# Routing of the gathered tile moved into the loop, and the early dot products read from PSUM behind their gathers

## The chip, the cores and the metric

The kernel runs on one core of one Trainium2 chip. The metric is the device time of one execution in microseconds, the median of three runs. The engines are named as the profile names them: PE (TensorE), DVE (VectorE), ACT (ScalarE), POOL (GpSimd), SP (which issues most transfers).

## The reference, cut to what matters

One layer of an encoder on 512 tokens of width 1024: a mixer (gating and banded attention), then a layer of 16384 experts of one row each, called PEER. All is float32. The change is in PEER:

```python
def block(xb):                                   # 128 tokens
    q = (xb @ w_query).reshape(128, 8, 2, 128)
    sc = einsum('thpd,hpkd->thpk', q, sub_keys)  # 8 heads, 2 halves, 128 keys
    s_top, i_top = top_k(sc, 16)
    cand = s_top[:, :, 0, :, None] + s_top[:, :, 1, None, :]
    cand_idx = i_top[:, :, 0, :, None] * 128 + i_top[:, :, 1, None, :]
    best, pos = top_k(cand.reshape(128, 8, 256), 16)
    eidx = take_along_axis(cand_idx.reshape(128, 8, 256), pos)
    g = softmax(best)
    h = gelu(einsum('thkd,td->thk', expert_u[eidx], xb))
    return einsum('thk,thkd->td', g * h, expert_v[eidx])
```

So each token chooses 16 of 16384 experts in each of 8 heads (the routing), and its output is a sum over 128 experts.

## The kernel before

The 512 tokens are four tiles of 128. The kernel treats the experts in two ways. For tiles 1 to 3 it multiplies all 16384 experts, in 64 chunks of 256: a first product (expert rows by tokens, then gelu, `first_products`, two units a chunk), a factor that is zero where an expert wasn't chosen (the gates), and a second product that accumulates in PSUM (`second_product`). For tile 0 it gathers the 128 chosen rows of each token from `expert_u` and `expert_v` with indirect transfers (`gather_u`, `gather_v`) and multiplies on DVE. The last 64 tokens of tile 3 are a mixture: their first products are left out of the matmuls and come from 64 gathers of `expert_u` (two heads of 64 tokens share one gather of 128 rows), the early dot products of `gather_early`. Their operand is `xbu`, their results go to `du`. Every float32 matrix product is three products of split operands: `load_split` loads `raw`, ACT rounds it to `hi`, DVE or POOL subtracts to get `lo`.

After the mixer (to about 236 us) the work runs in three stages:

1. Routing, one head at a time (`candidates`, `choose`): the query product and the scores on PE, then on DVE for each tile and half a `top16` (two rounds of the eight largest with their places), the candidate sums, another `top16` over 50 candidates, and a selection by predicated copies from `tree`, whose mask stands in PSUM. POOL makes the `lo` of the query weights, some small index operations and the copy `tree`. Each head also holds one chunk of first products. From the fourth head's pass on, three early gathers a pass are issued.
2. The gates stage: 48 steps of 8 tokens. A step makes two one-hot matrices: `bm` on DVE, multiplied by the gates on POOL, and `am` on DVE (even steps) or on ACT (odd ones). Two steps later PE multiplies them, ACT copies the result to `gst`, and every four steps 2 MB go to DRAM (`gd`). The remaining early gathers are spread over the first `SOON` = 28 steps, and units of the first product fill PE's time.
3. The loop over 64 chunks: the second product of chunk c, the first of c + 19, and tile 0's 256 gathers with their work on DVE, spread in proportion. The gates come back from `gd` as `gc`.

Instructions are written in program order; a scheduler then orders those of each engine by priority and by when its own model has their inputs ready, except PE's in the gates stage and the loop, which keep program order. Once built, every engine executes its list in order. A tile of a pool with n buffers waits until the last user of the one n back is done: the early gathers write `rowe`, with three buffers. PSUM has eight banks: two for `pu` (first products), six for `pa` (all others, six accumulators in the loop). In before, a dot product follows its gather at once:

Of the kernel before, what the change touches and what calls it, by code (L numbers as in the profile page):

```python
# [58 lines left out]
ROWE = 3  # L59
# [8 lines left out]
PRIO = 400  # L68
GB = 4
# [10 lines left out]
def hybrid_block(tc, x, ln1, w_in, gng, wsT, bsb, qkg, bias, w_out, ln2, wq, skT, uT, ud, vd, out):  # L80
    nc = tc.nc
    ctx = ExitStack()
    with ctx:
# [3 lines left out]
        ps_a = ctx.enter_context(tc.tile_pool(name="ps_a", bufs=6, space=PSUM))  # L87
# [343 lines left out]

        rt = ctx.enter_context(tc.tile_pool(name="rt", bufs=1, side="right"))
# [10 lines left out]
        xbu = gat.tile([P, D], F32, name="xbu")  # L443
        for i in range(P // UX):
            nc.sync.dma_start(xbu[i * UX:(i + 1) * UX, :], xbd[1, P - UX:, :])
# [4 lines left out]
        early = []  # L450

        def gather_early(n):
            for j in early[:n]:
                row = gat.tile([P, D], F32, name="rowe", tag="rowe", bufs=ROWE)
                nc.gpsimd.indirect_dma_start(out=row, out_offset=None, in_=ud,  # L455
                                             in_offset=bass.IndirectOffsetOnAxis(ap=eui[:, j:j + 1], axis=0))
                nc.vector.scalar_tensor_tensor(row, row, 1.0, xbu, op0=ALU.mult, op1=ALU.mult,  # L457
                                               accum_out=du[:, j:j + 1])
# [35 lines left out]

        routing = ExitStack()
        rq = routing.enter_context(tc.tile_pool(name="rq", bufs=1))
        bits = rq.tile([P, 6], U32, name="bits")
        for i in range(6):
            nc.vector.memset(bits[:, i:i + 1], 1 << i)
# [8 lines left out]

        def candidates(h):
# [4 lines left out]

            top = rq.tile([P, 2, TT, 2, TOPK], F32, name="top", tag="top", bufs=2)
            pos = rq.tile([P, TT, 2, TOPK], U32, name="pos", tag="pos", bufs=2)
# [10 lines left out]
            next(fill, None)  # L527
            for p2 in range(2):
# [4 lines left out]
                sc = rq.tile([P, TT, NK], F32, name="scr", tag="scr", bufs=2)  # L533
                nc.scalar.copy(sc, sp.rearrange("p (t n) -> p t n", n=NK))
# [6 lines left out]
            nc.gpsimd.tensor_copy(top[:, 1, :, 1, :], pos[:, :, 1, :])  # L541
            cand = rq.tile([P, 2, TT, NCAND], F32, name="cand", tag="cand", bufs=2)
            a = top.rearrange("p a t q r -> p (a t) q r")
            c = cand.rearrange("p a t n -> p (a t) n")
            for i, j in ROWS:
                m, n = j - i, NPAIR[i]
                full = [P, 2 * TT, m, n]
                nc.vector.tensor_tensor(c[:, :, POFF[i]:POFF[i] + m * n].rearrange("p c (m n) -> p c m n", n=n),
                                        a[:, :, 1, None, 0:n].to_broadcast(full),
                                        a[:, :, 0, i:j, None].to_broadcast(full), op=ALU.add)  # L550
            return cand

        def choose(h, cand):

            hs = slice(h * TOPK, (h + 1) * TOPK)
            best = gate[:, :, hs]
            tree = rq.tile([P, TT, TOPK, 32], F32, name="tree", tag="tree", bufs=1)
            nc.gpsimd.tensor_copy(tree, cand[:, 1, :, None, 0:32].to_broadcast([P, TT, TOPK, 32]))
            bpos = rq.tile([P, TT, TOPK], U32, name="bpos", tag="bpos", bufs=2)
            for t in range(TT):  # L560
                rep = rq.tile([P, NCAND], F32, name="rep2", tag="rep2", bufs=2)
                top16(best[:, t, :], bpos[:, t, :], cand[:, 0, t, :], rep)

            mask = ps_a.tile([P, 512], U32, name="mask", tag="pa")[:, 0:6 * TT * TOPK]
            nc.vector.tensor_tensor(mask.rearrange("p (l n) -> p l n", l=6),
                                    bpos.rearrange("p t k -> p (t k)")[:, None, :]
                                    .to_broadcast([P, 6, TT * TOPK]),
                                    bits[:, :, None].to_broadcast([P, 6, TT * TOPK]), op=ALU.bitwise_and)
            mask = mask.rearrange("p (l t k) -> p l t k", t=TT, k=TOPK)
            for i in reversed(range(6)):  # L570
                if i == 5:
                    n = NCAND - 32
                    other = cand[:, 1, :, None, 32:NCAND].to_broadcast([P, TT, TOPK, n])
                else:
                    n = 1 << i
                    other = tree[:, :, :, n:2 * n]
                nc.vector.copy_predicated(tree[:, :, :, 0:n],  # L577
                                          mask[:, i, :, :, None].to_broadcast([P, TT, TOPK, n]), other)
            nc.gpsimd.tensor_copy(eidx[:, :, hs], tree[:, :, :, 0])
# [5 lines left out]
        for h in range(NH + 1):  # L585
            if h < NH:
                cands.append(candidates(h))
            gather_early(EARLY)
            if h > 0:
                choose(h - 1, cands.pop(0))  # L590
# [6 lines left out]
        best = gate.rearrange("p t (h k) -> p (t h) k", k=TOPK)  # L597
        full = [P, TT * NH, TOPK]
        ex = rq.tile(full, F32, name="ex")
        nc.vector.tensor_tensor(ex, best, best[:, :, 0:1].to_broadcast(full), op=ALU.subtract)  # L600
        nc.scalar.activation(ex, ex, AF.Exp)
        zs = rq.tile([P, TT * NH], F32, name="zs")
        nc.vector.reduce_sum(zs, ex, axis=AX.X)
        nc.vector.reciprocal(zs, zs)
        nc.vector.tensor_tensor(best, ex, zs[:, :, None].to_broadcast(full), op=ALU.mult)
        nc.vector.tensor_copy(eint, eidx[:, 0, :])
# [65 lines left out]
        hots, gs = {}, {}  # L672
        with tc.manual_schedule(engines={mybir.EngineType.PE}):
            for n in range(steps + LEAD):
                if n < steps:
# [3 lines left out]
                    hots[n] = one_hots(gs[t], c, n % 2 == 1)  # L679
                    want = (len(early) + max(0, SOON - n) - 1) // max(1, SOON - n)  # L680
                    gather_early(want)
                    if c == per - LEAD - 2 and t + 1 < ND:
                        if t + 2 == ND:
                            gather_early(len(early))
                            weights_early()
# [8 lines left out]
                while filled < min(last, 2 * (NH * FILL + 1) + (last - 2 * (NH * FILL + 1)) * (n + 1) // SOON):  # L694
# [152 lines left out]
```

## Time and profile before

| | |
|---|---|
| median of three runs | 1576.74 us (1573.69 to 1576.75) |
| profiled execution | 1577.37 us, of which its span 1575.3 |
| mean granted clock of PE | 0.955 |
| busy: PE, DVE, ACT, POOL | 1415.6, 1173.5, 652.6, 687.4 us |
| transfers | 394.66 MB, mean 251 GB/s |

Times in the profile count from the span's start. Busy time counts a pipelined instruction to its modelled end, so neighbours can overlap, and the distance between two starts says more than a duration. An idle time is put down to what ended it.

### The profile page before, as it was taken

To read this page: it belongs to the slowest core of one execution; us is meant where nothing else is said; L and a number is where in the kernel's file an instruction comes from. 1 tells how busy PE (TensorE), PEld (TensorE's weight loads), DVE (VectorE), ACT (ScalarE), POOL (GpSimd) and SP (SyncE) were. 2 spreads that over 40 slices of the span, in tenths; PEclk is the share of its full clock that TensorE was granted. 3 is DMA by queue.
4 is the path that set the end of the run, shared out by engine and by line. 5 is a ranking of instruction groups with operands and counts; after the bars stand their busy time and mean duration, and the time that the engine had idled before them with its cause. 6 is when DMAs were issued, how large, how long until landed. Compare 5 with 4: busy or idle time off the path is not lost.

```text
span 1575.3 us, 21612 instructions
## 1 busy us (share of the span) xinstructions
PE 1415.6 (90%) x7801; PEld 1249.5 (79%) x7801; DVE 1173.5 (74%) x2257; ACT 652.6 (41%) x1118; POOL 687.4 (44%) x464
## 2 busy tenths in 40 slices
PE   7999999987627666969999999999999999999988
PEld 6886779976527556868898998989999898988866
DVE  4437455999998878645787888888788788868774
ACT  5457443322125446963343333333333343333321
POOL 0000035675457664631445455555445554525320
PEclk9999999999759788999999999999999999999999
DMA  5352244265247886677999999999999999978872
GB/s 175 106 174 68 94 160 141 94 219 164 94 134 225 274 263 199 190 229 279 346 337 351 339 344 338 349 328 343 352 337 336 354 341 337 336 278 306 336 255 98
DMA packets 161210, 394.66 MB, mean 251 GB/s; under 512 B 11920, under 2 KB 72336, under 8 KB 161104
## 3 DMA queue, kind: packets, MB, share of 16 engines
q1 hardware_dynamic: 64912, 199.25, 36.6%
q0 software_dynamic: 46432, 168.60, 29.3%
q10 hardware_dynamic: 49760, 25.45, 5.7%
q8 instruction: 61, 1.00, 0.3%
q14 instruction: 45, 0.37, 0.1%
HBM read 362.81 MB, written 30.41 MB: 250 GB/s over the span
## 4 chain that ended last, share of the span: by engine, by line
PE 53%; DVE 8%; DMA 7%; issue 4%; ACT 3%; POOL 2%; DVEq 0%; SPq 0%; POOLq 0%; ACTq 0%
PE pa L774 10%; PE pa L775 10%; PE pa L778 10%; PE pu L128 7%; PE pu L130 7%; PE pu L129 7%; DMA rowe<-in_ud,eui 4%; DMA gc<-gd 2%; DVE rowe L457 2%; DVE tree L577 1%; ACT am L649 1%; ACT gst L662 1%; PE pa L659 1%; POOL bm L645 1%; POOL rowe L455 1%
## 5 line engine op out<-in xcount | busy, mean ns | idle before, releaser
L112 ACT ACTIVATE hi<-raw 128x1024 fp32r<-128x1024 f32 x300 | 317.2, 1059 | 536.2 <-PE pu L129 197.8
L113 DVE TENSOR_TENSOR lo<-raw,hi 128x1024 fp32r<-128x1024 f32 x268 | 330.3, 1233 | 129.5 <-ACT hi L112 128.6
L130 PE MATMUL pu<-xch,lo 128*128 128x320 f32 x880 | 277.1, 315 | 35.3 <-DVE lo L113 35.3
L774 PE MATMUL pa<-hi,wh 128*128 128x512 f32 x768 | 301.5, 393 | 3.0 <-ACT wh L758 3.0
L775 PE MATMUL pa<-lo,wh 128*128 128x512 f32 x768 | 300.7, 391 | 0.0
L723 POOL DMA_INDIRECT row<-in_vd,eint x128 | 210.9, 1647 | 202.7 <-DVE acc L725 185.7
L128 PE MATMUL pu<-xch,hi 128*128 128x320 f32 x880 | 279.3, 317 | 11.2 <-ACT act L492 7.7
L712 POOL DMA_INDIRECT row<-in_ud,eint x128 | 179.2, 1400 | 236.0 <-DVE row L714 197.9
L129 PE MATMUL pu<-xcl,hi 128*128 128x320 f32 x880 | 276.8, 315 | 0.0
L778 PE MATMUL pa<-hi,wl 128*128 128x512 f32 x768 | 238.1, 391 | 7.3 <-DVE wl L759 4.2
L130 PEld LDWEIGHTS pu<-xch,lo 128*128 128x128 f32 x880 | 170.6, 194 | 37.0 <-DVE lo L113 37.0
L128 PEld LDWEIGHTS pu<-xch,hi 128*128 128x128 f32 x880 | 170.9, 194 | 13.9 <-ACT act L492 8.2
L778 PEld LDWEIGHTS pa<-hi,wl 128*128 128x128 f32 x768 | 144.6, 189 | 40.0 <-DVE wl L759 5.0
L129 PEld LDWEIGHTS pu<-xcl,hi 128*128 128x128 f32 x880 | 170.4, 194 | 1.9
L774 PEld LDWEIGHTS pa<-hi,wh 128*128 128x128 f32 x768 | 145.0, 189 | 32.6 <-ACT wh L758 3.2
L775 PEld LDWEIGHTS pa<-lo,wh 128*128 128x128 f32 x768 | 144.8, 189 | 28.8
L725 DVE SCALAR_TENSOR_TENSOR acc<-row,hw,acc 128x1024 f32<-128x1024 f32 x128 | 164.1, 1282 | 0.2
L714 DVE SCALAR_TENSOR_TENSOR row<-row,xb 128x1024 f32<-128x1024 f32 x128 | 155.7, 1218 | 0.0
L457 DVE SCALAR_TENSOR_TENSOR rowe<-rowe,xbu 128x1024 f32<-128x1024 f32 x64 | 105.2, 1652 | 27.9 <-DMA rowe<-in_ud,eui 27.5
L645 POOL TENSOR_TENSOR bm<-bm,gt 128x1024 f32<-128x1024 f32 x48 | 97.7, 2045 | 39.8 <-DVE bm L644 39.6
L659 PE MATMUL pa<-bm,am 128*128 128x128 f32 x768 | 94.7, 282 | 19.6 <-ACT am L650 9.4
L659 PEld LDWEIGHTS pa<-bm,am 128*128 128x128 f32 x768 | 91.9, 198 | 21.7 <-issue 11.7
(193 smaller groups left out, 2116.8 us busy)
## 6 DMA issues: line engine op xcount, KB each, us to landing
raw<-in_uT SPq DMA_DIRECT2D x128, 512.0 KB, 5.9
raw<-in_vd SPq DMA_DIRECT2D x128, 512.0 KB, 6.1
gd<-gst ACTq DMA_DIRECT2D x12, 2048.0 KB, 11.1
gc<-gd SPq DMA_DIRECT2D x32, 768.0 KB, 6.0
raw<-in_w_in SPq DMA_DIRECT2D x20, 512.0 KB, 4.5
raw<-in_wq SPq DMA_DIRECT2D x16, 512.0 KB, 3.4
raw<-in_w_out SPq DMA_DIRECT2D x8, 512.0 KB, 3.9
bt<-in_bias SPq DMA_DIRECT2D x8, 256.0 KB, 7.4
```

The lines of the kernel that those rows point to most:

```text
L112: nc.scalar.activation(hi, raw, AF.Copy)
L113: eng.tensor_tensor(lo, raw, hi.bitcast(F32), op=ALU.subtract)
L128: nc.tensor.matmul(ps, lh[0], rh[0], start=first, stop=False)
L129: nc.tensor.matmul(ps, lh[0], rh[1], start=False, stop=False)
L130: nc.tensor.matmul(ps, lh[1], rh[0], start=False, stop=last)
L659: nc.tensor.matmul(ps[:, i * P:(i + 1) * P], am[:, 4 * q + i, :], bm[:, 4 * q + i, :], start=True, stop=True)
L712: nc.gpsimd.indirect_dma_start(out=row, out_offset=None, in_=ud, in_offset=bass.IndirectOffsetOnAxis(ap=eint[:, j:j + 1], axis=0))
L723: nc.gpsimd.indirect_dma_start(out=row, out_offset=None, in_=vd, in_offset=bass.IndirectOffsetOnAxis(ap=eint[:, j:j + 1], axis=0))
L725: nc.vector.scalar_tensor_tensor(acc0, row, hw[:, j:j + 1], acc0, op0=ALU.mult, op1=ALU.add)
L774: nc.tensor.matmul(accs[t][half], wh[:, b, tok], w[b][0][:, ds_], start=first, stop=False)
L775: nc.tensor.matmul(accs[t][half], wh[:, b, tok], w[b][1][:, ds_], start=False, stop=False)
L778: nc.tensor.matmul(accs[t][half], wl[:, b, tok], w[b][0][:, ds_], start=False, stop=last)
```

## The change

Tile 0's routing leaves the first stage. There `candidates` and `choose` now treat tiles 1 to 3 only; tile 0's scores are copied by ACT to `s0` and stored to DRAM (`s0d`). The code of the routing is cut into functions (`keys`, `best_keys`, `pairs`, `choose`, `softmax`), and `route_gathered` calls them inside the loop, for four heads at a time, at chunks 0 and 8. The small index operations go from POOL to DVE.

The operand of the early dot products, `xbu`, is copied to two PSUM banks (`px`), which later are accumulators of the loop; `pa` has four banks from the routing on. `gather_early` only issues gathers; `dots_early` issues the dot products, one pass later in the routing, two steps later in the gates stage. `rowe` has four buffers. In the gates stage ACT builds `am` in odd steps only up to step 28, and four units of the first product are put ahead of the stage (`BRIDGE`).

```diff
-ROWE = 3
+ROWE = 4
+LAGE = 2
+BRIDGE = 4
+ROUTE = 8
...
+        psa_ctx.close()
+        ps_x = ctx.enter_context(tc.tile_pool(name="ps_x", bufs=1, space=PSUM))
+        ps_a = ctx.enter_context(tc.tile_pool(name="ps_b", bufs=4, space=PSUM))
...
-        xbu = gat.tile([P, D], F32, name="xbu")
+        xbu = px()
+        row = gat.tile([P, D], F32, name="rowe", tag="rowe", bufs=ROWE)
...
+        nc.scalar.copy(xbu[:, 0:512], row[:, 0:512])
+        nc.scalar.copy(xbu[:, 512:], row[:, 512:])
...
-                nc.vector.scalar_tensor_tensor(row, row, 1.0, xbu, op0=ALU.mult, op1=ALU.mult,
-                                               accum_out=du[:, j:j + 1])
+                rows.append((j, row))
             del early[:n]
+            issued.append(rows)
+
+        def dots_early(lag):
+            while len(issued) > lag:
+                for j, row in issued.pop(0):
+                    nc.vector.scalar_tensor_tensor(row, row, 1.0, xbu, op0=ALU.mult, op1=ALU.mult,
+                                                   accum_out=du[:, j:j + 1])
...
-            nc.gpsimd.tensor_copy(eu[P - UX:P, js], eidx[P - UX:P, TT - 1, h * TOPK:(h + 1) * TOPK])
-            nc.gpsimd.tensor_copy(eui[:, js], eu[:, js])
+            nc.vector.tensor_copy(eu[P - UX:P, js], eidx[P - UX:P, TT - 1, h * TOPK:(h + 1) * TOPK])
+
+        def ready_early(h):
+            js = slice(h // 2 * TOPK, (h // 2 + 1) * TOPK)
+            nc.vector.tensor_copy(eui[:, js], eu[:, js])
...
-                sc = rq.tile([P, TT, NK], F32, name="scr", tag="scr", bufs=2)
-                nc.scalar.copy(sc, sp.rearrange("p (t n) -> p t n", n=NK))
-                for t in range(TT):
-                    rep = rq.tile([P, NK], F32, name="rep", tag="rep", bufs=2)
-                    top16(top[:, 0, t, p2, :], pos[:, t, p2, :], sc[:, t, :], rep)
+                sc = rq.tile([P, ND, NK], F32, name="scr", tag="scr", bufs=2)
+                nc.scalar.copy(sc, sp.rearrange("p (t n) -> p t n", n=NK)[:, GT:, :])
+                nc.scalar.copy(s0[:, p2, :], sp[:, 0:NK])
+                for t in range(ND):
+                    best_keys(rq, top, pos, t, p2, sc[:, t, :])
+            nc.scalar.dma_start(s0d[h], s0.rearrange("p a n -> p (a n)"))
...
-            nc.gpsimd.tensor_scalar(top[:, 1, :, 0, :], pos[:, :, 0, :], float(NK), None, op0=ALU.mult)
-            nc.gpsimd.tensor_copy(top[:, 1, :, 1, :], pos[:, :, 1, :])
...
         for h in range(NH + 1):
+            if h > 2 and h % 2 == 1:
+                ready_early(h - 3)
+            dots_early(1)
+            gather_early(EARLY)
             if h < NH:
                 cands.append(candidates(h))
-            gather_early(EARLY)
...
+        for _ in range(BRIDGE):
+            next(fill)
...
-                    hots[n] = one_hots(gs[t], c, n % 2 == 1)
+                    dots_early(LAGE)
+                    hots[n] = one_hots(gs[t], c, n % 2 == 1 and n < SOON)
...
+        def route_gathered(b):
+
+            n = NH // 2
+            sc = ep.tile([P, n, 2, NK], F32, name="sc0", tag="sc0", bufs=1)
+            nc.sync.dma_start(sc.rearrange("p h a n -> p h (a n)"), s0d[b * n:(b + 1) * n].rearrange("h p a -> p h a"))
+            top, pos = keys(ep, n)
+            for h in range(n):
+                for p2 in range(2):
+                    best_keys(ep, top, pos, h, p2, sc[:, h, p2, :])
+            hs = slice(b * n * TOPK, (b + 1) * n * TOPK)
+            best, to = (x[:, 0, hs].rearrange("p (h k) -> p h k", k=TOPK) for x in (gate, eidx))
+            mask = ep.tile([P, 6 * n * TOPK], U32, name="mask", tag="mask", bufs=1)
+            choose(ep, *pairs(ep, top, pos, n), n, best, to, mask)
+            softmax(ep, best, n)
+            nc.vector.tensor_copy(eint[:, hs], eidx[:, 0, hs])
...
-        accs = [[pa() for _ in range(2)] for _ in range(ND)]
+        acx = px()
+        accs = [[acx[:, 0:512], acx[:, 512:]]] + [[pa() for _ in range(2)] for _ in range(ND - 1)]
...
+                if c % ROUTE == 0 and c < 2 * ROUTE:
+                    route_gathered(c // ROUTE)
```

How the order moves on the engines that wait or are waited for. First DVE in the gates stage (`rowe` with a number is one gathered row; the dot product reads it; `bm` and `am` are one-hots, `lo` an operand of PE). Before:

```order
L644 TENSOR_TENSOR bm_4355<-iota_k_74,pa_4108 128x1024
L652 TENSOR_TENSOR am_4354<-iota_k_74,pa_4108 128x1024
L457 SCALAR_TENSOR_TENSOR rowe_4359,du_1996<-rowe_4359,xbu_1991 128x1024
L457 SCALAR_TENSOR_TENSOR rowe_4362,du_1996<-rowe_4362,xbu_1991 128x1024
L457 SCALAR_TENSOR_TENSOR rowe_4391,du_1996<-rowe_4391,xbu_1991 128x1024
L644 TENSOR_TENSOR bm_4379<-iota_k_74,pa_4108 128x1024
```

And after:

```order
L481 SCALAR_TENSOR_TENSOR rowe_4527,du_2006<-rowe_4527,px_1998 128x1024
L689 TENSOR_TENSOR bm_4401<-iota_k_74,pa_4130 128x1024
L697 TENSOR_TENSOR am_4400<-iota_k_74,pa_4130 128x1024
L689 TENSOR_TENSOR bm_4457<-iota_k_74,pa_4130 128x1024
L481 SCALAR_TENSOR_TENSOR rowe_4580,du_2006<-rowe_4580,px_1998 128x1024
L481 SCALAR_TENSOR_TENSOR rowe_4582,du_2006<-rowe_4582,px_1998 128x1024
L481 SCALAR_TENSOR_TENSOR rowe_4626,du_2006<-rowe_4626,px_1998 128x1024
L689 TENSOR_TENSOR bm_4489<-iota_k_74,pa_4130 128x1024
```

The dots stand in groups behind several one-hots and read `px`, the PSUM tile. On POOL, which issues the gathers and multiplies `bm` by the gates `gt`, the same rows stand so before:

```order
L455 DMA rowe_4359<-in_ud,eui_1995 128x1024
L455 DMA rowe_4362<-in_ud,eui_1995 128x1024
L455 DMA rowe_4391<-in_ud,eui_1995 128x1024
L645 TENSOR_TENSOR bm_4290<-bm_4290,gt_4112 128x1024
L645 TENSOR_TENSOR bm_4355<-bm_4355,gt_4112 128x1024
```

And after:

```order
L690 TENSOR_TENSOR bm_4370<-bm_4370,gt_4134 128x1024
L472 DMA rowe_4580<-in_ud,eui_2005 128x1024
L472 DMA rowe_4582<-in_ud,eui_2005 128x1024
L472 DMA rowe_4626<-in_ud,eui_2005 128x1024
L472 DMA rowe_4628<-in_ud,eui_2005 128x1024
L690 TENSOR_TENSOR bm_4401<-bm_4401,gt_4134 128x1024
L690 TENSOR_TENSOR bm_4457<-bm_4457,gt_4134 128x1024
```

Gather 4580 is now issued ahead of product 4401, and its dot stands on DVE behind one-hots 4401 and 4457. Last, DVE at the start of the loop (`act`, `wl`: operands of the second product; `sc_5928`: tile 0's scores). Before:

```order
L757 TENSOR_TENSOR act<-act,gc 128x320 x4
L759 TENSOR_TENSOR wl<-act,wh 128x2x320 x2
L764 TENSOR_TENSOR wl<-gc,wh 128x2x2x32
L113 TENSOR_TENSOR lo<-raw,hi 128x1024 x2
L757 TENSOR_TENSOR act<-act,gc 128x320 x4
```

And after:

```order
L825 TENSOR_TENSOR act<-act,gc 128x320 x4
L827 TENSOR_TENSOR wl<-act,wh 128x2x320
L832 TENSOR_TENSOR wl<-gc,wh 128x2x2x32
L530 MAX top<-sc_5928 128x8 x2
L531 MAX_INDEX pos<-top,sc_5928 128x8
L532 MATCH_REPLACE rep<-top,sc_5928 128x128
```

The rounds of block 0 stand between the operands of the first chunks, and the first dot of tile 0 stands behind the whole block.

More of the change, by code (lines that the diff above doesn't have):

```diff
@@ L449, in hybrid_block @@
         dots = gat.tile([P, NH // 2, 2, TOPK], F32, name="dots")
-        early = []
+        early, issued = [], []
         def gather_early(n):
+            rows = []
             for j in early[:n]:
@@ L493, in first_products @@
                 yield
+        bits = rt.tile([P, 6], U32, name="bits")
+        for i in range(6):
+            nc.vector.memset(bits[:, i:i + 1], 1 << i)
         routing = ExitStack()
         rq = routing.enter_context(tc.tile_pool(name="rq", bufs=1))
-        bits = rq.tile([P, 6], U32, name="bits")
-        for i in range(6):
-            nc.vector.memset(bits[:, i:i + 1], 1 << i)
+        s0d = dram.tile([NH, P, 2 * NK], F32, name="s0d")
         def top16(val, pos, src, scratch):
@@ new lines, in choose @@
+        def choose(pool, cand, tree, n, best, to, mask):
+            bpos = pool.tile([P, n, TOPK], U32, name="bpos", tag="bpos", bufs=2)
+            for t in range(n):
+                rep = pool.tile([P, NCAND], F32, name="rep2", tag="rep2", bufs=2)
+                top16(best[:, t, :], bpos[:, t, :], cand[:, 0, t, :], rep)
+            nc.vector.tensor_tensor(mask.rearrange("p (l n) -> p l n", l=6),
+                                    bpos.rearrange("p t k -> p (t k)")[:, None, :]
+                                    .to_broadcast([P, 6, n * TOPK]),
+                                    bits[:, :, None].to_broadcast([P, 6, n * TOPK]), op=ALU.bitwise_and)
+            mask = mask.rearrange("p (l t k) -> p l t k", t=n, k=TOPK)
+            for i in reversed(range(6)):
+                if i == 5:
+                    m = NCAND - 32
+                    other = cand[:, 1, :, None, 32:NCAND].to_broadcast([P, n, TOPK, m])
+                else:
+                    m = 1 << i
+                    other = tree[:, :, :, m:2 * m]
+                nc.vector.copy_predicated(tree[:, :, :, 0:m],
+                                          mask[:, i, :, :, None].to_broadcast([P, n, TOPK, m]), other)
+            nc.vector.tensor_copy(to, tree[:, :, :, 0])
@@ new lines, in softmax @@
+        def softmax(pool, best, n):
+            full = [P, n, TOPK]
+            ex = pool.tile(full, F32, name="ex")
+            nc.vector.tensor_tensor(ex, best, best[:, :, 0:1].to_broadcast(full), op=ALU.subtract)
+            nc.scalar.activation(ex, ex, AF.Exp)
+            zs = pool.tile([P, n], F32, name="zs")
+            nc.vector.reduce_sum(zs, ex, axis=AX.X)
+            nc.vector.reciprocal(zs, zs)
+            nc.vector.tensor_tensor(best, ex, zs[:, :, None].to_broadcast(full), op=ALU.mult)
@@ L513, in candidates @@
             nc.sync.dma_start(skt, skT[:, 2 * h:2 * h + 2, :])
-            top = rq.tile([P, 2, TT, 2, TOPK], F32, name="top", tag="top", bufs=2)
-            pos = rq.tile([P, TT, 2, TOPK], U32, name="pos", tag="pos", bufs=2)
+            top, pos = keys(rq, ND)
             qts = []
@@ L542, in candidates @@
[L542 to L579, printed above, removed]
@@ L582, in hybrid_block @@
+            return pairs(rq, top, pos, ND)
         for _ in first_products(0, nc.vector, True):
@@ L596, in hybrid_block @@
                 nc.gpsimd.tensor_copy(xcl, xbl[:, :, T0:T0 + NDU])
[L597 to L606, printed above, removed]
+        softmax(rq, gate[:, GT:, :].rearrange("p t (h k) -> p (t h) k", k=TOPK), ND * NH)
+        ready_early(NH - 2)
         routing.close()
@@ L693, in hybrid_block @@
                         store(m * TC // TG, st)
-                while filled < min(last, 2 * (NH * FILL + 1) + (last - 2 * (NH * FILL + 1)) * (n + 1) // SOON):
+                while filled < min(last, begun + (last - begun) * (n + 1) // SOON):
                     next(fill)
```

36 lines of the change are left out of this document (33 added, 3 removed).

## The prediction

> **What bounds the kernel now.** I read the page's busy shares and slices first, then cut the span into stages, then the chain and the groups inside the stages where TensorE idles.
>
> ```profile
> span 1575.3 us, 21612 instructions
> PE 1415.6 (90%) x7801; PEld 1249.5 (79%) x7801; DVE 1173.5 (74%) x2257; ACT 652.6 (41%) x1118; POOL 687.4 (44%) x464
> PE   7999999987627666969999999999999999999988
> DVE  4437455999998878645787888888788788868774
> ```
>
> TensorE is full except in slices 8 to 17, and there VectorE (DVE) is full instead. The stages show it in numbers (columns: stretch, its length, busy time and count of each engine, granted clock, DMA share, GB/s):
>
> ```profile
> 236.00:345.00 109.00, 105.42 (x597) 95.40 (x596) 90.62 (x445) 37.93 (x55) 71.31 (x48) 0.99 0.50 153
> 345.00:464.50 119.50, 65.19 (x311) 56.79 (x311) 112.74 (x500) 21.81 (x33) 63.86 (x53) 0.76 0.38 122
> 464.50:606.00 141.50, 93.41 (x617) 90.30 (x616) 117.98 (x132) 77.94 (x175) 96.84 (x60) 0.84 0.79 253
> 606.00:711.40 105.40, 80.56 (x609) 78.91 (x609) 60.66 (x56) 78.83 (x182) 51.97 (x30) 0.92 0.69 206
> 711.40:1486.00 774.60, 773.84 (x4161) 693.71 (x4162) 618.29 (x801) 290.10 (x411) 373.91 (x245) 1.00 0.91 332
> ```
>
> The first two are the routing, the next two the gates stage (its first one-hot starts at 464.5; the early gathers end near 606), the fifth the loop, from its first product at 711.4. The loop is bound by TensorE (773.8 of 774.6 us), with DVE at 80% and the DMA engines at 91%. From 345 to 711 TensorE works 239 of 366 us. Its work is the same after the change, so time is won only there, and can be lost in the loop.
>
> The routing is bound by DVE: 112.7 of 119.5 us. TensorE alone would need less. It made the first heads 19.8 us apart (evacuations of the query product of two heads) before DVE held it back:
>
> ```profile
> 241.61 0.59 ACT L524 COPY qt<-pa 128x512 f32<-128x512 f32 x1 [4.09 <-PE pa L130]
> 261.39 0.59 ACT L524 COPY qt<-pa 128x512 f32<-128x512 f32 x1 [4.24 <-PE pa L130]
> 251.75 1.19 ACT L534 COPY scr<-pa 128x512 f32<-128x512 f32 x2
> ```
>
> The last of eight heads would have its scores at 251.75 + 7 x 19.8 = 390 us.
>
> In the first part of the gates stage the gathers of the early dot products bind. Here are all 64 dot products and gathers, then rows in order of time (in brackets the idle time ahead and what ended it):
>
> ```profile
> L457 DVE SCALAR_TENSOR_TENSOR rowe<-rowe,xbu 128x1024 f32<-128x1024 f32 x64 | 105.2, 1652 | 27.9 <-DMA rowe<-in_ud,eui 27.5
> L455 POOL DMA_INDIRECT rowe<-in_ud,eui x64 | 81.0, 1265 | 58.4 <-DVE rowe L457 41.2 <-issue 5.5 <-DVE top L506 2.9
> ...
> 513.24 2.92 DVE L457 SCALAR_TENSOR_TENSOR rowe<-rowe,xbu 128x1024 f32<-128x1024 f32 x1
> 519.72 1.22 DVE L457 SCALAR_TENSOR_TENSOR rowe<-rowe,xbu 128x1024 f32<-128x1024 f32 x1 [3.56 <-DMA rowe<-in_ud,eui]
> 513.16 1.91 POOL L645 TENSOR_TENSOR bm<-bm,gt 128x1024 f32<-128x1024 f32 x1
> 521.23 0.94 POOL L455 DMA_INDIRECT rowe<-in_ud,eui  x1 [3.81 <-DVE rowe L457]
> ```
>
> It is a ring: three row buffers, a dot that stands right behind its gather and waits for the landing, and a next gather that waits for the dot. A dot needs 1.22 us, but 2.92 when a GpSimd (POOL) product starts beside it (513.16); that makes the mean 1.65. In the stretch of 141.5 us stand 39 of them, 3.6 us each:
>
> ```profile
> L457 DVE SCALAR_TENSOR_TENSOR rowe<-rowe,xbu 128x1024 f32<-128x1024 f32 x39 | 65.4, 1688 | 22.6 <-DMA rowe<-in_ud,eui 22.2
> ```
>
> From 606 on, the one-hot matrices built on ScalarE hold the steps back: DVE idles 19.9 us ahead of its own one-hots.
>
> ```profile
> L644 DVE TENSOR_TENSOR bm<-iota_k,pa 128x1024 f32<-128x1024 f32 x25 | 30.2, 1217 | 19.9 <-PE pa L659 19.8
> ```
>
> **The change part by part**, on the DVE path from 251.75 to 711.4.
>
> *Routing of three tiles instead of four.* The pitch of a top-16 round is 1.17 us over 128 keys and 0.78 over 50 candidates:
>
> ```profile
> 405.77 0.28 DVE L503 MAX8 top<-scr 128x8 f32<-128x128 f32 x1
> 406.94 0.29 DVE L503 MAX8 top<-scr 128x8 f32<-128x128 f32 x1
> ...
> 441.81 0.20 DVE L503 MAX8 gate<-cand 128x8 f32<-128x50 f32 x1
> 442.59 0.20 DVE L503 MAX8 gate<-cand 128x8 f32<-128x50 f32 x1
> ...
> L577 DVE COPY_PREDICATED tree<-mask,tree 128x1024 f32<-128x1024 uint32 (+4 forms) x40 | 26.4, 660 | 0.1
> L577 DVE COPY_PREDICATED tree<-mask,cand 128x1152 f32<-128x1152 uint32 x8 | 12.7, 1590 | 0.3
> L548 DVE TENSOR_TENSOR cand<-top 128x64 f32<-128x64 f32 (+5 forms) x56 | 11.5, 277 | 2.1 <-POOL top L541 1.9
> ```
>
> 16 and 8 rounds go: 18.7 + 6.2 us. Selection and candidates (50.6 us) keep their number of instructions at three quarters of the width; a full quarter is 12.6 us, and I take 10. Together -35.
>
> *Small operations from POOL to DVE.* Three a head and two for each of four index sets, 32 in all. The nearest DVE row is a conversion of 128x128:
>
> ```profile
> 532.50 0.21 DVE L621 CAST ei<-eidx 128x128 int32<-128x128 f32 x1
> ```
>
> Less than 0.21 us each, so +3 to +7; I take +5.
>
> *Operand of the dots in PSUM.* The trace has no dot with a PSUM operand. Nearest are the one-hot above, which reads PSUM beside the same POOL products (1217 ns), and the dots of the loop, with both operands in SBUF and no POOL product beside them:
>
> ```profile
> L714 DVE SCALAR_TENSOR_TENSOR row<-row,xb 128x1024 f32<-128x1024 f32 x128 | 155.7, 1218 | 0.0
> ```
>
> I take 1.22: 64 x (1.65 - 1.22) = -27. The ends are 0 (the delay stays) and -27. The two copies that fill PSUM run on ScalarE (35% and 18% busy in the routing) long ahead of the first dot; exposed they would cost two copies of 0.59 us. ScalarE's two small evacuations more a head, which set the fourth tile's scores aside, lie in the same idle time. [...]
>
> *Dots two steps behind their gathers, four buffers.* DVE's 27.9 us of waiting for landings should mostly go. What is late next is the gather itself: it still waits for the dot four rows back, and one-hot products queue behind it on POOL. I leave 8 us: -20; ends 0 and -27.9.
>
> *One-hots after step 28 all on DVE.* ScalarE builds 10 fewer, DVE 10 more at a pitch under 1.21: +11.5, in place of the 19.9 us of idle: together -8.5, at worst +11.5. The next limit there is the gate store: 2 MB for every four steps, from two buffers. With steps of 2.4 us a buffer is filled in 9.7 us and lands in 11.1, so the two allow one in 10.4 us, 0.7 more than DVE needs:
>
> ```profile
> gd<-gst ACTq DMA_DIRECT2D x12, 2048.0 KB, 11.1
> rowe<-in_ud,eui POOLq DMA_INDIRECT x64, 5.7
> row<-in_ud,eint POOLq DMA_INDIRECT x128, 7.5
> ```
>
> So far -35 + 5 - 27 - 20 - 8.5 = -85.5. The gates stage moves nearly the same bytes (DMA share 0.79) in less time, so landings grow and I give back 10: **-75**. With all waits kept it is -35 + 5 - 27 + 11.5 = -45.5. Two accumulator pools of four buffers in place of six, one of them held by the transposed indices of a tile, cost nothing as long as ScalarE empties a bank in 0.6 us; I know no row that prices more, and it lies inside the 10.
>
> *Four units of the first product as a bridge.* They run on TensorE while DVE ends the routing, where TensorE idles anyway. One unit more stands ahead of the loop: 24 matmuls, three in 0.45 us, so 3.5 us less for the loop: **-3.5**.
>
> ```profile
> 741.26 0.31 PE L128 MATMUL pu<-xch,hi 128*128 128x320 f32 x1
> 741.71 0.31 PE L128 MATMUL pu<-xch,hi 128*128 128x320 f32 x1
> 742.09 1.22 DVE L714 SCALAR_TENSOR_TENSOR row<-row,xb 128x1024 f32<-128x1024 f32 x1
> ```
>
> *Routing in the loop.* Two blocks, each 8 key rounds, 4 candidate rounds and a selection for four heads: 8 x 1.17 + 4 x 0.78 + about 6 + 1.5 = 20 us for DVE at least, 27 with waits between. DVE is idle 20% of the loop, but the first gather of tile 0 now waits for block 0. Before, the first dot starts 31 us into the loop (742.09), and finds its row landed. After, block 0 stands behind products of the first chunks; I put its end at 45 to 50 us and a landing of 7.5 behind. That is some 24 us later. The 256 gathers of the loop stand 2.9 us apart on average (774.6 - 31 over 256), so 8 of them, 0.5 MB each, have to be caught up where the DMA is 91% busy. Dots that wait in DVE's order hold up the operands behind them: **+10**, between 0 and +30. The second block feeds gathers that are due late, and hides; its one copy on POOL stands among the gathers in that queue and waits for DVE's candidates, and the gathers behind it wait too, which is part of the +30. The scores go out in eight stores on ScalarE's queue and come back in two loads on SP's, 1 MB each way, beside some 330 GB/s in the loop.
>
> Sum: -75 - 3.5 + 10 = -68.5. The profiled execution took 1577.4 us, 2.1 us around its span, 0.6 above the median shown: 1577.4 - 68.5 = 1509. The terms' ends give 1577.4 - 85.5 - 3.5 = 1488 and 1577.4 - 45.5 - 3.5 + 30 = 1558.
>
> **The rivals.**
> - *Gathers still bind.* POOL's order alternates gathers that wait for dots with the products that DVE and TensorE wait for; landings get longer. All waits stay, -45.5 in place of -75: 1538. For it: DMA share 0.79. Against: a dot now has two steps of other DVE work ahead of it. 0.15.
> - *The loop takes more back.* Both blocks show on TensorE: 27 and 12 us in place of 10, so 1538. For it: DMA at 91%; against: 156 us of DVE idle time in the loop. 0.10.
> - *PSUM doesn't do what it is put there for*, and a dot still stops beside a POOL product: +27, 1536. The one-hot's 1217 ns speaks against. 0.08.
> - *Slower than before.* Tile 0's gathers, started late, never catch up with a saturated DMA, and each of the 256 dots and accumulations makes DVE, and TensorE behind it, wait. The win of 78.5 ahead of the loop and its shorter work is eaten at 0.31 us each; at 0.35 it is +90, 1589. Against: six row buffers, and DMA demand that falls again near the end. 0.05.
>
> **How the numbers follow.** My own case has 0.62, the rivals 0.38. Differences of 0.2% (3 us) are about what a measurement of this kernel can tell. All but the last rival end faster: 0.94, none within 0.2% but a tail of 0.01, slower 0.05. The time is my own case's, 1509. The range takes in the three faster rivals, goes a little under the sum's lower end and leaves out the last rival and the last 8 us of the upper end, which all terms would have to reach together: 1482 to 1550.
>
> **What would show it.** The first one-hot near 435 to 440 in place of 464.5, the first loop product near 636. Mean dot of 1.25 us, and DVE's wait for its rows below 10 us in all. DVE above 90% busy from 252 to the last one-hot. In the loop, TensorE idle 10 us around the third to sixth chunk, and none later. The forecast is wrong if POOL's gathers keep idling 40 us for dots, if the stage ahead of the loop is as long as before at a DMA share above 0.9, or if TensorE has idle time all through the loop.

## Result, and the profile after

The changed kernel takes 1524.62 us (median of four runs, 1521.59 to 1526.82), the kernel before 1576.74: a ratio of 0.9666, 95% interval 0.9637 to 0.9695. It is 52 us faster, where 68.5 were forecast; 1524.6 lies within the range of 1482 to 1550. The profiled execution took 1521.59, of which its span 1519.8. The head of its page and its busy slices:

```profile
span 1519.8 us, 21632 instructions
PE 1401.5 (92%) x7801; PEld 1236.7 (81%) x7801; DVE 1174.2 (77%) x2342; ACT 628.8 (41%) x1052; POOL 659.5 (43%) x434
...
PE   7999999989738679869999999999999999999988
...
DVE  5437454879999888759998888888887888867774
```

TensorE's thin slices are still there, but fewer, and DVE's full slices too. For the comparison I cut both spans at the same marks, which are the first top-16 round on DVE, the first one-hot, the end of the last one-hot, the first product of the loop and the end (columns: stretch, its length, busy time and count of PE, weight loads, DVE, ACT, POOL, then granted clock, DMA share, GB/s). Before:

```profile
252.40:464.50 212.10, 154.21 (x817) 137.69 (x816) 203.32 (x944) 53.16 (x78) 125.51 (x96) 0.86 0.42 134
464.50:681.70 217.20, 155.60 (x1109) 151.53 (x1109) 169.07 (x175) 141.22 (x328) 142.15 (x84) 0.87 0.73 228
681.70:711.40 29.70, 18.36 (x119) 17.68 (x117) 9.57 (x13) 15.55 (x30) 6.65 (x6) 0.87 0.85 268
711.40:1575.30 863.90, 851.05 (x4488) 755.73 (x4488) 668.77 (x864) 312.01 (x441) 385.30 (x252) 0.99 0.88 319
```

and after:

```profile
251.00:453.50 202.50, 163.38 (x908) 147.62 (x906) 181.23 (x798) 61.31 (x105) 109.77 (x72) 0.93 0.55 178
453.50:640.30 186.80, 151.98 (x1119) 148.17 (x1119) 161.06 (x176) 116.66 (x252) 123.09 (x77) 0.91 0.82 260
640.30:660.90 20.60, 4.71 (x41) 4.52 (x41) 1.75 (x5) 4.06 (x8) 0.74 (x1) 0.72 0.77 241
660.90:1519.80 858.90, 848.22 (x4464) 751.30 (x4464) 705.04 (x1099) 315.33 (x443) 398.07 (x258) 0.99 0.86 319
```

The routing gave 10 us, the gates stage 30, the handover to the loop 9, the loop with its tail 5. The loop is the surprise: DVE works 36 us more in it (705.0 against 668.8), and TensorE idles less, 10.7 us against 12.8.

What became of the DVE path shows best if each instant from the first round to the last one-hot is given to one owner: to the instruction that runs (each counted from the end of the one before it), or, where DVE idles, to what ended the wait. Worked out from the two traces:

| us of DVE's time | before | after | difference | forecast |
|---|---|---|---|---|
| top-16 rounds | 98.6 | 74.3 | -24.3 | -24.9 |
| candidates and selection | 60.6 | 43.1 | -17.5 | -10 |
| small index operations | (POOL) | 16.8 | +16.8 | +5 |
| waits for POOL's index operations | 1.9 | 0 | -1.9 | 0 |
| waits for scores after the first | 0 | 6.2 | +6.2 | 0 |
| early dot products | 102.5 | 74.4 | -28.1 | -27 |
| waits for gathered rows | 27.5 | 21.1 | -6.4 | -20 |
| one-hots | 82.5 | 94.0 | +11.5 | +11.5 |
| waits of the one-hots for TensorE | 20.6 | 10.3 | -10.3 | -20 |
| `lo` operands of first products, and waits for `hi` | 27.4 | 40.4 | +13.0 | 0 |
| all else | 7.7 | 8.6 | +0.9 | 0 |

That sums to -40, where the forecast column has -85.5 (10 of them given back unplaced). The first round starts 1.4 us earlier, and the handover is 9.0 us shorter: `lo` operands of the last first products, which stood in the handover before, now stand among the one-hots. With 5.0 from the loop this makes the 55.5 us between the two spans. The rows of the profile behind the largest differences, after the change (idle time ahead and its cause behind the bar):

```profile
L481 DVE SCALAR_TENSOR_TENSOR rowe<-rowe,px 128x1024 f32<-128x1024 f32 x64 | 77.1, 1216 | 21.2 <-DMA rowe<-in_ud,eui 21.1
L481 DVE SCALAR_TENSOR_TENSOR rowe<-rowe,px 128x1024 f32<-128x1024 f32 x32 | 38.7, 1215 | 13.1 <-DMA rowe<-in_ud,eui 13.0
L472 POOL DMA_INDIRECT rowe<-in_ud,eui x64 | 68.6, 1072 | 55.8 <-DVE rowe L481 41.1 <-issue 6.9 <-DVE gate L533 4.2
L689 DVE TENSOR_TENSOR bm<-iota_k,pa 128x1024 f32<-128x1024 f32 x48 | 58.1, 1216 | 10.4 <-PE pa L704 10.3
L488 DVE COPY eu<-eidx 64x16 f32<-64x16 f32 x4 | 7.3, 1836 | 0.1
L547 DVE TENSOR_SCALAR top<-pos 128x48 f32<-128x48 uint32 x8 | 5.1, 634 | 0.0
```

The second row is of the routing alone (236 to 453.5 us): 13.0 of the 21.1 us of waits for rows stand there, 7.8 of them for the first row of all, and 8.1 in the gates stage. Before, 22.2 of the 27.5 stood in the gates stage and 5.3 in the routing.

The dot takes 1216 ns, as the prediction took it. But the gathers on POOL still idle 41.1 us for dots (41.2 before), which the prediction had named as a sign against itself. And a copy of 16 numbers a partition takes 1836 ns.

### The profile page after: what moved, and what is told of

It reads as the page before. It is cut to its first block, busy times and chain, and to the rows that moved or that the text cites. A ratio compares the mean times of both kernels' runs of the same rounds, so it can differ in the third digit from the quotient of the medians.

```text
span 1519.8 us, 21632 instructions
## 1 busy us (share of the span) xinstructions
PE 1401.5 (92%) x7801; PEld 1236.7 (81%) x7801; DVE 1174.2 (77%) x2342; ACT 628.8 (41%) x1052; POOL 659.5 (43%) x434
## 4 chain that ended last, share of the span: by engine, by line
PE 63%; DVE 17%; DMA 9%; issue 6%; ACT 3%; POOL 2%; DVEq 0%; SPq 0%; POOLq 0%
PE pu L132 8%; PE pu L134 8%; PE pu L133 8%; PE pa L842 6%; PE pa L843 6%; PE pa L846 6%; DMA rowe<-in_ud,eui 3%; DMA gc<-gd 3%; PE px L846 3%; PE px L842 3%; PE px L843 3%; PE pa L704 2%; PE pa L132 2%; PE pa L134 2%; PE pa L133 2%
## 5 line engine op out<-in xcount | busy, mean ns | idle before, releaser
L132 PE MATMUL pu<-xch,hi 128*128 128x320 f32 x880 | 273.6, 311 | 4.3 <-ACT act L518 4.2
L842 PE MATMUL pa<-hi,wh 128*128 128x512 f32 x512 | 201.1, 393 | 0.0
L843 PE MATMUL pa<-lo,wh 128*128 128x512 f32 x512 | 200.6, 392 | 0.0
L846 PE MATMUL pa<-hi,wl 128*128 128x512 f32 x512 | 158.8, 391 | 0.4 <-DVE wl L832 0.4
L781 DVE SCALAR_TENSOR_TENSOR row<-row,xb 128x1024 f32<-128x1024 f32 x128 | 155.7, 1219 | 2.4 <-DMA row<-in_ud,eint 2.4
L704 PE MATMUL pa<-bm,am 128*128 128x128 f32 x768 | 101.0, 292 | 36.3 <-DVE bm L689 12.2
L825 DVE TENSOR_TENSOR act<-act,gc 128x320 f32<-128x320 f32 x128 | 54.8, 486 | 88.2 <-DMA gc<-gd 88.2
L842 PE MATMUL px<-hi,wh 128*128 128x512 f32 x256 | 100.9, 394 | 15.9 <-ACT wh L826 15.9
L846 PEld LDWEIGHTS pa<-hi,wl 128*128 128x128 f32 x512 | 96.5, 189 | 21.6 <-DVE wl L832 1.1
L842 PEld LDWEIGHTS pa<-hi,wh 128*128 128x128 f32 x512 | 96.9, 189 | 20.6
L843 PEld LDWEIGHTS pa<-lo,wh 128*128 128x128 f32 x512 | 96.9, 189 | 20.6
```

Source lines behind the costliest of these rows:

```text
L132: nc.tensor.matmul(ps, lh[0], rh[0], start=first, stop=False)
L704: nc.tensor.matmul(ps[:, i * P:(i + 1) * P], am[:, 4 * q + i, :], bm[:, 4 * q + i, :], start=True, stop=True)
L842: nc.tensor.matmul(accs[t][half], wh[:, b, tok], w[b][0][:, ds_], start=first, stop=False)
L843: nc.tensor.matmul(accs[t][half], wh[:, b, tok], w[b][1][:, ds_], start=False, stop=False)
L846: nc.tensor.matmul(accs[t][half], wl[:, b, tok], w[b][0][:, ds_], start=False, stop=last)
```

## The experiments

All are edits of the changed kernel. Ratios are to the kernel before, run beside them; 0.001 is 1.6 us. The changed kernel's own is 0.9666, and an interval is about 0.003 wide to each side, so differences below 5 us between two variants are not told apart by time alone; where I use them, it is by the trace. One trace has an uncertainty of its own: the run with more work in the loop (below) has the changed kernel's order on DVE but for the last few instructions ahead of the loop, and yet waits 17.8 us for rows there where the changed kernel waits 21.1, and has 45.2 us of candidates and selection where that has 43.1. In these two sums, differences of 3 us between two traces show nothing.

### The fourth row buffer

```diff
-ROWE = 4
+ROWE = 3
```

> The changed kernel with three row buffers for the early gathers in place of four; the operand stays in PSUM and the dots stay two steps behind. If the gathers wait for the dot that frees their buffer, DVE's 21.1 us of waiting for rows (changed kernel) go up by about a third, +7 us: 1532. If the rows wait for landings alone, the buffer count does nothing: 1525 within 3.

Measured: 1543.54 us, ratio 0.9802 (0.9777 to 0.9826), 19 us slower than the changed kernel. The dots' row, whose wait doubles:

```profile
L481 DVE SCALAR_TENSOR_TENSOR rowe<-rowe,px 128x1024 f32<-128x1024 f32 x64 | 77.4, 1215 | 42.2 <-DMA rowe<-in_ud,eui 42.1
```

The first theory holds and was far too small: waits of 42.1 us against 21.1. They are longer than before the change (27.5), but hardly in the gates stage, 24.2 against 22.2; the rest stands in the routing, 17.9 against 5.3, where DVE, with three tiles to route, comes to its dots sooner.

### The operand in PSUM

```diff
-        xbu = px()
+        xbu = gat.tile([P, D], F32, name="xbu")
```

(with `ROWE = 3`, and the operand loaded into `xbu` itself, without ScalarE's two copies)

> The operand of the early dot products back in SBUF, and three row buffers as in the run beside it (four do not fit then). Theory 1: each dot stops again beside a POOL product, 64 x (1.65 - 1.22) = 27 us over the kernel with three row buffers and the operand in PSUM, about 1557, with dots of a mean near 1.65 us. Theory 2: the dots get longer, but DVE waited some 21 us for the rows anyway, and the longer dots only fill these waits: +6 to +10, about 1540, and the waits for rows fall to near 10.

Measured: 1566.88 us, ratio 0.9941 (0.9918 to 0.9963), 23 us above the run with three buffers and the operand in PSUM.

```profile
L478 DVE SCALAR_TENSOR_TENSOR rowe<-rowe,xbu 128x1024 f32<-128x1024 f32 x64 | 103.9, 1634 | 40.4 <-DMA rowe<-in_ud,eui 40.3
```

Theory 1: the mean dot goes from 1215 to 1634 ns, 27 us in all, the waits for rows stay (40.3 against 42.1), and most of it is on the path.

### The lag

```diff
-            dots_early(1)
             gather_early(EARLY)
+            dots_early(0)
...
-                    dots_early(LAGE)
                     hots[n] = one_hots(...)
...
                     gather_early(want)
+                    dots_early(0)
```

> Each dot product follows its gather at once, in the routing and in the gates stage; four buffers and the PSUM operand stay. Theory 1: the lag took only the 6 us of row waits off that the traces differ by (27.5 to 21.1): 1531. Theory 2 (the prediction's term of 20): without the lag the waits come back in full, 1545. Theory 3: the gather's wait for the dot four rows back is the ring's limit, and the lag makes that later: no change or a gain, 1520 to 1525.

Measured: 1529.28 us, ratio 0.9703 (0.9672 to 0.9734).

```profile
L481 DVE SCALAR_TENSOR_TENSOR rowe<-rowe,px 128x1024 f32<-128x1024 f32 x64 | 76.9, 1214 | 21.8 <-DMA rowe<-in_ud,eui 21.8
```

Without the lag the waits for rows are the same, 21.8 against 21.1 us. By time the lag is worth some 5 us, with intervals that overlap; the trace puts them elsewhere, in candidates and selection (47.9 against 43.1 us, of which 2 are within the uncertainty of a trace), and their cause is open. So theory 1 gave the time, and theory 3 the waits, which don't change: with four buffers, what DVE waits for is not set by how far behind its gather a dot stands in the program. With three, no run takes away the lag alone. The nearest pair is the kernel before and the run with the operand in SBUF, with dots of 1652 and 1634 ns; they differ in other parts too. In the gates stage they wait 22.2 us without the lag and 22.3 with it.

### Five row buffers

```diff
-ROWE = 4
+ROWE = 5
-            ff = gp.tile([P, 2, NH * TOPK], F32, name="ff", tag="ff", bufs=1)
+            ff = ii.bitcast(F32)
```

(and `eint` and `hw` move from `rt` to `ep`)

> Five row buffers for the early gathers (room for the fifth comes from a cast in place in the gates stage and from two tiles moved to the loop's pool). Theory 1: the buffers are the ring's limit; DVE waited 42.1 us for rows with three and 21.1 with four, so about 10 with five: 1514. Theory 2: what is left are landings that DVE's order asks for too early, which no buffer shortens: 1522 to 1526.

Measured: 1515.70 us, ratio 0.9625 (0.9590 to 0.9660), 9 us below the changed kernel by the medians, 6 by the ratios.

```profile
L479 DVE SCALAR_TENSOR_TENSOR rowe<-rowe,px 128x1024 f32<-128x1024 f32 x64 | 76.5, 1214 | 10.4 <-DMA rowe<-in_ud,eui 10.2
```

Theory 1, in the waits (10.2 us for about 10) and nearly in the time (1514 expected): 42.1, 21.1 and 10.2 us of waiting with three, four and five buffers. In the gates stage alone it is 24.2, 8.1 and 4.2. More than half of the 10.2 is one wait, 5.8 us for the first gather of all, which stands in the routing of the other two as well.

### The small index operations

Back on POOL:

```diff
-            nc.vector.tensor_copy(eu[P - UX:P, js], ...)
+            nc.gpsimd.tensor_copy(eu[P - UX:P, js], ...)
```

(and so the copies `eui`, `eidx`, and the two operations on `pos` in the routing)

> The small index operations of the routing (three a head, two for each of four sets of early indices) back on POOL; those of the blocks in the loop stay on DVE. Theory 1: on DVE they cost 16.8 us, since 15 of the 36 stand until a running POOL product ends; back on POOL they cost DVE some 2 to 4 us of waiting: 1512. Theory 2: POOL works its list in order, and they hold up the gathers behind them as much as DVE wins: 1522 to 1530.

Measured: 1520.48 us, ratio 0.9658 (0.9633 to 0.9683). DVE is rid of the 16.8 us, but waits 7.4 us more for rows and 3.1 more for scores:

```profile
L481 DVE SCALAR_TENSOR_TENSOR rowe<-rowe,px 128x1024 f32<-128x1024 f32 x64 | 76.6, 1215 | 28.7 <-DMA rowe<-in_ud,eui 28.5
L530 DVE MAX8 top<-scr 128x8 f32<-128x128 f32 x48 | 12.9, 281 | 27.3 <-ACT scr L621 27.3
```

(24.2 us for scores in the changed kernel; 18 of either stand ahead of the first.) In time it is a draw with the changed kernel, between the two theories. Ten of the 32 small operations start during a POOL subtraction and take 0.54 to 2.41 us, where the other 22 take 0.15 to 0.25; the 15 of 36 that were expected are not in the trace. Why so small an operation is so slow on DVE, the changed kernel's rows in order of time show; a POOL subtraction (a `lo`) starts at 283.46, the copy 0.06 us later, and both end together at 285.9:

```profile
283.46 2.40 POOL L117 TENSOR_TENSOR lo<-raw,hi 128x1024 fp32r<-128x1024 f32 x1 [0.27 <-ACT hi L116]
283.52 2.38 DVE L488 COPY eu<-eidx 64x16 f32<-64x16 f32 x1
```

The test is the same numbers in another form:

```diff
-            nc.vector.tensor_copy(eui[:, js], eu[:, js])
+            nc.vector.reduce_max(eui[:, js], eu[:, js, None], axis=AX.X)
```

(and `eu` likewise)

> The copy of 64x16 early indices and their conversion to integers (eu, eui: eight DVE instructions) written as a maximum over one element, which gives the same numbers; all else as changed. Theory 1: these two forms stand until a running POOL product ends (10.1 us in the changed kernel, up to 2.4 us each) because of their form, and a reduction does not: each takes 0.3 us or less whatever POOL does, 1524.6 - 8 = 1517. Theory 2: they wait for something else, and last as long as before: 1525. Theory 3: they get short, and DVE waits the longer for the rows behind them: 1521 to 1525.

Measured: 1522.46 us, ratio 0.9656 (0.9621 to 0.9691). At the same place, beside the same POOL subtraction, the reduction takes 0.17 us:

```profile
286.22 2.40 POOL L117 TENSOR_TENSOR lo<-raw,hi 128x1024 fp32r<-128x1024 f32 x1 [0.27 <-ACT hi L116]
286.28 0.17 DVE L488 TENSOR_REDUCE eu<-eidx 64x16 f32<-64x16 f32 x1
```

So here the form alone makes the difference, 2.38 us against 0.17. The eight operations fall from 10.1 us to below 2, all small operations from 16.8 to 7.1; the waits for rows grow by 3.7 us, little more than two traces of one order differ by, and those for scores by 2.9, and the time gains little if anything. Theory 3.

### Tile 0 routed in the first stage

```diff
-                sc = rq.tile([P, ND, NK], F32, name="scr", tag="scr", bufs=2)
+                sc = rq.tile([P, TT, NK], F32, name="scr", tag="scr", bufs=2)
...
-                if c % ROUTE == 0 and c < 2 * ROUTE:
-                    route_gathered(c // ROUTE)
```

> Tile 0 routed in the first stage with the other three, nothing of the routing in the loop; all else as changed. Theory 1: the fourth tile adds to DVE what the traces of before and after differ by, 24.3 us of rounds and 17.5 us of selection, and the loop gives nothing back, since TensorE already waits only 5 us there: 1524.6 + 42 = 1566. Theory 2: the longer routing covers the waits that DVE has there in the changed kernel (13.0 us for rows, 6.2 us for scores): 1524.6 + 42 - 19 = 1548. Theory 3 (the prediction's term): the loop pays 10 us for its two blocks, which come back: 10 us below the one or the other.

Measured: 1539.15 us, ratio 0.9769 (0.9737 to 0.9802): 15 us slower by the medians, 16 by the ratios. Its four stretches:

```profile
253.70:462.10 208.40, 164.76 (x907) 147.97 (x905) 202.87 (x973) 58.48 (x86) 102.64 (x63) 0.91 0.43 143
462.10:657.30 195.20, 153.74 (x1118) 150.13 (x1118) 171.56 (x196) 119.53 (x255) 131.08 (x87) 0.90 0.85 275
657.30:680.40 23.10, 6.36 (x40) 6.17 (x40) 2.33 (x7) 3.98 (x8) 5.87 (x6) 0.66 0.72 230
680.40:1537.50 857.10, 847.18 (x4464) 752.22 (x4464) 667.09 (x862) 309.59 (x437) 383.19 (x252) 0.99 0.87 318
```

DVE has 38.7 us more of rounds and selection ahead of the loop, and waits less: 13.8 us for rows against 21.1, none for scores against 6.2, 6.2 for TensorE against 10.3, 3.2 for `hi` against 7.0; the small operations, with other neighbours, take 12.4 us against 16.8. The loop and tail take 857.1 us against 858.9 with the routing in them, so by these two traces the routing in the loop costs 2 us. That is nearest theory 2, and with still more of the waits covered. By the time alone theory 2 less the 10 us of theory 3 (1538) would fit better; the loop's 2 us speak against it.

### More work for DVE in the loop

```diff
                 for p2 in range(2):
-                    best_keys(ep, top, pos, h, p2, sc[:, h, p2, :])
+                    for _ in range(3):
+                        best_keys(ep, top, pos, h, p2, sc[:, h, p2, :])
```

> The key rounds of both blocks in the loop are done three times over (same numbers): 2 x 8 x 1.17 = 18.7 us more for DVE in each block, 37.4 us in all; nothing else differs from the changed kernel. DVE's idle time in the changed kernel is 17.5 us from 650 to 750 us and 14.2 us from 750 to 900. Theory 1: DVE's idle time there is real slack, and only what exceeds it stops TensorE: 1524.6 + 6 = 1531. Theory 2: the operands of the products go first and the dots just come later: 1525. Theory 3: the blocks stand in DVE's list ahead of operands that TensorE needs at once, so most of it shows: 1550 to 1562.

Measured: 1549.48 us, ratio 0.9853 (0.9820 to 0.9886): 25 us slower by the medians, 29 by the ratios, 22 in the profiled spans. First the changed kernel where its second block runs (743 to 799 us), then this one's whole loop and the stretch in which its second block ends (at 869):

```profile
750.00:800.00 50.00, 49.53 (x275) 44.32 (x274) 49.52 (x126) 21.03 (x30) 22.24 (x16) 1.00 0.88 314
```

```profile
661.60:1542.20 880.60, 855.37 (x4464) 752.40 (x4464) 742.49 (x1355) 314.03 (x443) 398.56 (x258) 0.99 0.83 311
850.00:900.00 50.00, 47.67 (x255) 41.72 (x256) 50.00 (x97) 19.11 (x28) 25.45 (x19) 1.00 0.88 316
```

In the changed kernel DVE is busy 49.5 of 50 us around the second block, and TensorE loses 0.5. So the first 36 us of routing are nearly free (2 us, by the run before) and the next 37 cost 22 to 29: TensorE waits for `lo` (14.8 us in the loop against 1.0). That is theory 3: the blocks stand ahead of operands that TensorE needs, and most of the added work shows (1550 to 1562 expected, met within the uncertainty). The loop's slack was nearly used up by the change.

### One-hots on ScalarE to the end, and the bridge

```diff
-                    hots[n] = one_hots(gs[t], c, n % 2 == 1 and n < SOON)
+                    hots[n] = one_hots(gs[t], c, n % 2 == 1)
```

> ScalarE builds the odd steps' one-hots to the end of the gates stage again. Theory 1: DVE loses 10 one-hots, 11.5 us, but waits for TensorE and ScalarE in their place, as it did before (20.6 us against 10.3): within 3 of 1524.6. Theory 2: the last 20 steps are bound by DVE alone, and the stage gets shorter: 1514. Theory 3: ScalarE, which also empties the accumulators of only four banks, falls behind: 1535.

Measured: 1524.73 us, ratio 0.9677 (0.9646 to 0.9709), no different. But the pieces differ:

```profile
629.50:651.20 21.70, 19.26 (x139) 18.64 (x138) 5.27 (x9) 12.07 (x26) 1.90 (x1) 1.00 0.91 272
651.20:1521.30 870.10, 849.57 (x4464) 752.21 (x4464) 707.97 (x1102) 317.65 (x447) 403.51 (x258) 0.99 0.85 319
```

DVE has 10 one-hots and about 9 us of `lo` less ahead of the last one-hot, waits 21.2 us for TensorE against 10.3, and the loop's first product stands at 651.2, 9.7 us earlier than in the changed kernel. The loop then takes 870.1 us against 858.9, and gives it back. The added loss has a place: from 100 to 250 us into the loop TensorE idles 8.3 us, against 1.2 in the changed kernel, mostly for DVE's `lo` and ScalarE's gelu. Theory 1 has the time; the way is theory 2 with a loss behind it that no theory named. The bridge:

```diff
-BRIDGE = 4
+BRIDGE = 0
```

> No units of the first product ahead of the gates stage; as many as before spread over its steps. Theory 1: 4 units of 24 matmuls, 14 us of TensorE, move into the gates stage, where TensorE idles anyway, and the loop does one unit more: 1524.6 + 3.5 = 1528. Theory 2: DVE's four subtractions for them (4 x 1.2 us) leave the routing, and the gates stage, which waits for TensorE 10 us, waits longer: 1530 to 1535.

Measured: 1526.68 us, ratio 0.9686 (0.9654 to 0.9717), 2 to 3 us slower, as theory 1 has it, and within the uncertainty.

### Two versions

The first joins five buffers and the reductions. The second adds ScalarE's one-hots to the end and `ROUTE = 16`, to see whether the loop's loss goes when the second block is moved away from the first.

> Five row buffers and the reductions for the early indices together. Sum of the two runs beside before (0.9625 and 0.9656 against 0.9666): 1513 to 1516. If the waits for rows that ate the shorter index operations go with the fifth buffer, DVE keeps most of their 9.7 us: 1508.

> As the version beside it, and ScalarE builds the odd one-hots to the end of the gates stage, and the second block of tile 0's routing stands at chunk 16 of the loop in place of 8. Theory 1: the 9.7 us that these one-hots won ahead of the loop were lost again in the loop because DVE was full where the second block stood; spread out, the loop keeps them: 1505. Theory 2: the loss in the loop has another cause: 1514 to 1518, as without both.

Measured: 1513.10 us, ratio 0.9619 (0.9597 to 0.9640), and 1509.00 us, ratio 0.9576 (0.9550 to 0.9602). Both beat both kernels, though the first's interval just touches the changed kernel's. The first is the sum of its parts and not the 1508 us: its waits for rows are 13.1 us, not less than with five buffers alone. The second lies between its two theories. Its last stretch:

```profile
639.60:1507.80 868.20, 848.92 (x4464) 750.90 (x4464) 707.49 (x1102) 318.01 (x447) 401.27 (x258) 1.00 0.86 320
```

Its loop starts 8.5 us earlier than the first version's (648.1) and is still 6 us longer (868.2 against 862.1). So the place of the second block accounts for a part of the loss at most. In the same stretch, 100 to 250 us into the loop, TensorE still idles 7.0 us (1.1 in the first version). What lengthens the loop there when it starts earlier is left open.

## Why the prediction was right, and where its steps failed

The bound was read rightly: 50 of the 55 us between the spans were won ahead of the loop, and the loop stayed TensorE's. The second largest term was right in size and cause. The **PSUM operand** was priced at -27: the dots' time fell by 28.1, and taking the operand back cost 23. A dot with its operand in PSUM takes 1216 ns in the mean, against 1219 for the loop's dots with both operands in SBUF. The longest of the 64 takes 1.27 us, though about a third of them run beside a POOL product or subtraction; before, with the operand in SBUF, the longest took 5.52.

Five terms were mis-sized.

- **Dots two steps behind, four buffers: -20, "the waits should mostly go".** The waits fell by 6.4. That is the sum of two: in the gates stage, where the prediction had looked, they fell by 14 (22.2 to 8.1), and in the routing they grew by 8 (5.3 to 13.0), since DVE with three tiles comes to its dots sooner (the first starts at 313.7 us in place of 324.5); with tile 0 routed in the first stage they are 0 there. The prediction gave the work to the lag, and the runs give it to the buffer: no lag changes the waits by 0.7 us, one buffer less by 21. The prediction's own sentence on what is late next, that the gather waits for the dot four rows back, was the limit and not a remainder.
- **Routing of three tiles: -35.** DVE's work fell by 41.8, more than priced: the 50.6 us that the prediction took a quarter of leave out the products that make the masks (13.7 us before, 9.2 after). But undoing it costs only 16 us. As DVE finishes sooner, it waits for scores and rows that it had found ready. The prediction knew when TensorE alone would have the scores (19.8 us a head) and did not carry it into the sum.
- **Small operations on DVE: +5.** They take 16.8 us, because ten of the 32 stand until a POOL subtraction ends. The nearest row, a conversion at 0.21 us, had been taken where it met none. In time it matters little, since shorter ones make DVE wait (the two runs above).
- **One-hots after step 28: -8.5.** They cost 11.5 and save 10.3 of waiting: nothing, as the run with ScalarE's one-hots shows, though there the gain ahead of the loop was lost in it.
- **Routing in the loop: +10.** It costs 2 us by the run without it: with the unit moved ahead (-3.5) the forecast had +6.5, measured is -5.0. Block 0 ends 42 us into the loop (45 to 50 forecast) and the first dot of tile 0 stands at 707.7, 47 us into it, 16 later than before; the gathers catch up without TensorE waiting.

So the first three signs named were met in part: first one-hot 453.5 in place of 435 to 440, first product of the loop 660.9 in place of 636, mean dot 1.22. The two on DVE were not: its waits for rows are 21 us in place of 10, and it is busy 342 of 389 us, 88%, up to the last one-hot. Nor was the one in the loop: TensorE is busy all of its first 99 us, where 10 us of idle time were expected, and loses 1.2 in the 100 behind. Of the signs against it, POOL's idle time for dots was met (41.1 us), and it goes with the term that failed, the waits for rows; with five buffers it is 32.8. Two misses went opposite ways, 25 us too much won ahead of the loop and 11 too much lost in it, so it is in part luck that the time came within 16 us. Of the rivals, "gathers still bind" (1538) came a little nearer than the forecast itself, 13 us against 16: the waits for rows and of the one-hots did not stay whole, but fell only from 48 to 31 us. The rival that is slower needed late gathers in the loop to cost TensorE 0.31 us a dot; none shows in the loop, which got shorter.

## What to carry to other kernels

Savings on the engine that binds don't add: each microsecond taken off makes the next limit (here scores, rows, the products of the one-hots) show, so price a part by what the other waits in that stage leave, and by undoing it: the seven parts taken back here, one run each (the operand on top of the buffer), come to some 60 us beside the 52 of all together. In a ring of transfer, use and next transfer, count the buffers first; standing further behind in program order (0.7 us of waits) did nothing that a fourth and fifth buffer did (21 and 11). Idle time of a second engine in a loop bound by another is a real place for work, but measure how much is left: 36 us went in for some 2, and of the next 37 more than half showed.

## What the runs showed of the hardware

Ten of the 32 small operations that the change puts on DVE start during a POOL subtraction of two SBUF tensors, and each ends within 0.1 us of its end: a copy of 64x16 takes up to 2.41 us and else 0.18, a conversion of 128x16 up to 1.38 and 0.16 where no POOL subtraction runs, a 128x48 product with a constant up to 1.92 and else 0.18. A reduction over one element, of the same data and beside the same POOL subtraction, takes 0.17. The prediction had seen DVE held up beside POOL in the dots (2.92 us for one of 1.22) and did not look for it in the small operations.
